# Spectra finished in PSUM: more matmuls and fewer vector steps in the S5 and Hyena stages

## The chip, the cores and the metric

The kernel runs on one core of a Trainium2 chip, which has eight. A core has five engines: PE (TensorE, matrix products, which load their weights in records called PEld), DVE (VectorE), ACT (ScalarE), POOL (GpSimd) and SP (SyncE, which issues most transfers). They run on their own and wait for one another by semaphores; each works off its own instructions strictly in order. Matrix products write to PSUM, from which DVE and ACT read; everything else is in SBUF. The metric is device time in microseconds (us), the median of several runs; profiles come from one execution that the hardware profiler recorded.

## What is computed

Two networks of two layers each run one after the other. Two of their mixers concern the change.

S5 is a diagonal linear recurrence over 512 tokens, 64 groups of 16 features with 64 complex states each:

```
u  = (h @ w_in).reshape(L, 64, 16)
ab = exp((a_re + i a_im) dt);  bb = (ab - 1) / a * b
s[t] = ab * s[t-1] + bb u[t]                 # complex, per group
y  = Re(c s) + d u;  z = gelu(y) @ w_glu
```

Hyena convolves with long filters that a small network of sines makes, scaled by their 1-norms:

```
hid  = sin(freq * (sin(freq * (emb @ w1 + b1)) @ w2 + b2))
h    = (hid @ w3 + b3) * exp(-t * |deltas|)          # forward and backward filters, 2 of each
kern = concat(fwd, 0, reversed(bwd[1:]))             # bwd at lag 0 is left out
k_f  = rfft(kern / sum(|kern|))
for o in range(2):
    z = parts[o + 1] * (irfft(rfft(z) * k_f[o]) + skip[o] * z)
```

## The kernel before

Work is float32 throughout. The projections split each operand into a high and a low part and add three products, in lines 191 to 193; these are most of PE's time. The kernel is written as Python that emits instructions; the order in which it emits them is the order in which each engine runs them, apart from what the framework moves when it places tiles.

**S5** (`s5`, `s5_block`). Eight blocks of 128 features. A block is cut into stages with a letter each: powers of lambda times B and C (`F`, `C`, on POOL through `powers`, tiles tm and pw), a table of unit rotations (`E`, on POOL through `rotation`: four products tm of 128x512, two sums into E), local kernels and the skip term (`Y`, `Z`), chunk inputs on PE (`L`), rotation, scan and rotation back on DVE (`I`, `J`, `K`, tiles rp and rq), outputs on PE (`O`, `U`). A round emits the stages in the order of the string ORDER, and AHEAD says how many blocks a stage runs ahead. The small letters a to h in ORDER are stages of the Hyena filters: two filters a round are worked off between the S5 stages, so that engines idle for the one have the other. S5 rounds run from about 60 to 297 us.

**Filters** (`filters`, stages in `one`). For each of 8 blocks of channels and 2 orders, hid times the sum and the difference of the forward and backward weights (fwpm, made on DVE) gives f + g and f - g in two banks; DVE multiplies them by the decay (ff). At lag 0 only the forward filter counts: three steps on one partition put half the sum into both (lines 1710 to 1712). The 1-norm comes from the larger of the absolute values (fab), summed by PE (line 1723). The skip term is a diagonal matrix fdg, made on DVE and added by PE (line 1734). Then `spectrum` runs, and SP stores the result fX to DRAM.

**`spectrum`** takes four residues (token modulo 4) of 128 channels and gives eight sums: cosine and sine sums of 128 frequencies and their three mirror images. Eight matmuls with the tables dft give the sums of each residue in a pair of banks. ACT copies one bank to spb; DVE makes bank + spb and bank - spb (spt); four more steps of 128x256 combine these into the eight images, on POOL for the filters (fX) and on DVE in Hyena (X). For the filters, whose cosine and sine inputs differ, four matmuls in a third bank give a correction, with a second copy on ACT and a step on DVE.

**Hyena** (`hyena`, `long_conv`), 1942 to 2250 us. PE projects (lines 191 to 193); ACT and DVE do a short convolution; then 8 chains (one for each block of channels, with two convolutions each, so 16 in all) run, two at a time, taken forward by `step` between the projections. A convolution (`long_conv`) is: spectrum X, product with the stored spectrum K (Y and pm; one of the products on POOL), four steps spt<-Y, four steps into a tile that is again named X, and eight inverse matmuls with idft (line 1787). POOL also makes the low parts wl of the projection weights here.

Of the kernel before, what the change touches and what calls it, by code (L numbers as in the profile page):

```python
# [9 lines left out]
F32 = mybir.dt.float32  # L10
# [32 lines left out]
# Stages of the S5 blocks (capitals and w, p, q) and of the Hyena filters among them (a to e, g, h), in the order in  # L43
# which a round emits them; how many blocks a stage is ahead of the round; blocks projected before the first round.
# [5 lines left out]
class Kern:  # L50
# [11 lines left out]
    def psum(self, banks, pairs=0):  # L62
        """PSUM of a phase: single banks and pairs of banks."""
# [36 lines left out]
    def filler(self, ctx, work, banks, pairs=0):  # L100
        """Work emitted in steps among that of a phase; work(pool) is a generator."""
# [51 lines left out]
    def act_table(self, name, after):  # L153
        """Load a table set, after an activation."""
# [60 lines left out]
    def params(self, room, name, groups):  # L215
        """Vectors given as rows of 128, at most 128 of them to a group: loads, then transposes into one tile."""
# [45 lines left out]
    # The operand of a projection is split without 1/rms, which is applied to its output; so it is ready as soon as  # L262
    # the residual is. Sums of squares come out per token, tokens on partitions.
# [27 lines left out]
    def stat_close(self, n=4):  # L291
        """1/rms, [token of block, block]"""
# [6 lines left out]
    def rsqrt(self, r, x):  # L299
        """With a Newton step: the square root is a table's."""  # L300
# [8 lines left out]
    def replicate(self, r4, ps=None):  # L309
        """[P, n] to n * 128 columns, the same on all partitions"""  # L310
# [11 lines left out]
    def ready(self, x, gain, dst):  # L322
        """Split x times gain."""
# [8 lines left out]
    def prepare(self, xT, gain, pool):  # L332
        """For the projections of the next stage: called with each feature block as its residual is final."""
# [16 lines left out]
    def prepare_stat(self, xT):  # L350
        """The statistics alone."""
# [10 lines left out]
    def load_x(self, src, lp):  # L362
        """Input tokens as t = 4 c + j, in halves of the features"""
# [8 lines left out]
    def prepare_x(self, raws, lp):  # L372
        """The residual in natural order into DRAM, the operand in order (j, c)."""
# [61 lines left out]
    def s5_params(self, pp, sp, raw, braw, craw):  # L435
        """Per-state numbers in layout [(g2 p), gp]; B and C in [(g2 p), gp, h]."""
# [13 lines left out]
        # exponentials of a_re dt and four times it; sines and cosines of theta and of 4 theta times 1, 2, 4 ... 64  # L450
# [18 lines left out]
        # f = (lambda - 1) / a  # L469
# [18 lines left out]
        sn, cs, _ = angles(4, 7, self.t([P, 2048], F32, "ssm_b_re", 1, sp).rearrange("p (i c) -> p i c", i=4))  # L488
        # bbar [P, 2, gp, h]
# [14 lines left out]
        # c [P, 2, gp, h]  # L504
# [9 lines left out]
        # powers of lambda, up and down  # L514
        up, down = self.t([P, 2, 32, 5], F32, "up", 1, pp), self.t([P, 2, 32, 4], F32, "down", 1, pp)
        V.memset(up[:, 0, :, 0:1], 1.0)
        V.memset(up[:, 1, :, 0:1], 0.0)
        V.tensor_copy(up[:, :, :, 1], lam)
        u1, u2 = self.t([P, 2, 32], F32, "u1", 1, sp), self.t([P, 2, 32], F32, "u2", 1, sp)
        for i in range(2, 5):  # L520
# [4 lines left out]
        for i in range(4):  # L525
            self.act(down[:, :, :, i], up[:, :, :, 3 - i], AF.Copy)
# [3 lines left out]
        for n in (16, 8):  # L530
            tab = self.t([P, 2, 32, n], F32, f"tab{n}", 1, pp)
            q1, q2 = (room[:, 1024 * (n == 8) + i * S :][:, :S].rearrange("p (c q m) -> p c q m", c=2, q=32) for i in range(2))
            eng = Pl if n == 16 else V
            if n == 8:
                yield
            Pl.memset(tab[:, 0, :, 0:1], 1.0)
            Pl.memset(tab[:, 1, :, 0:1], 0.0)
            m = 1
            while m < n:
                sh = [P, 2, 32, m]  # L540
                bc = lambda x: x[:, b].unsqueeze(1).unsqueeze(3).to_broadcast(sh)
                with self.tc.issue_after(self.scaled) if n == 8 else nullcontext():
# [8 lines left out]
    def exp(self, sp, out, x, out1=None):  # L551
        """exp to float32's accuracy: 2^k times a polynomial on [-ln 2 / 2, ln 2 / 2]; out1 takes exp - 1"""
# [22 lines left out]
    def sin_cos(self, room, r, sn, cs, cm):  # L575
        """r in [-pi, pi]: sine by its series after folding into [-pi / 2, pi / 2]; cm = cos - 1 = -2 sin^2(r / 2)"""
# [16 lines left out]
    def s5_block(self, sp, fb, slot, sS):  # L593
        """The stages of a block of features"""
# [6 lines left out]
        capr, capi, fpr, fpi, bd = slot  # L601
        b = {}

        # C lambda^tau, tau <= 4, or B lambda^(3 - j), spread block-diagonally over the two groups of the partitions
        def powers(src, tab, n, dst):
            pw = self.t([P, 2, 4 * 5 * 16], F32, "pw", 1, p["pool"])[:, :, : 64 * n].rearrange("p c (q t h) -> p c q t h", q=4, h=16)
            m = [[self.t((P, S), F32, f"tm{i}{c}", 1, p["pool"])[:, : 64 * n].rearrange("p (q t h) -> p q t h", q=4, h=16)
                  for c in range(2)] for i in range(2)]
            sh = [P, 4, n, 16]
# [4 lines left out]
            self.tt(pw[:, 0], m[0][0], m[1][1], ALU.subtract, eng1)  # L614
            self.tt(pw[:, 1], m[0][1], m[1][0], ALU.add, eng1)
# [5 lines left out]
        def powers_f():  # L621
            powers(p["bb"], p["down"], 4, (fpr, fpi))
# [1431 lines left out]
```

## Time and profile before

| | us |
|---|---|
| median of 3 runs | 2312.88 (2309.42 to 2322.04) |
| span of the profiled execution | 2317.0 |
| S5 rounds, first two (60 to 134) | 74 |
| S5 rounds, middle three (134 to 233) | 99 |
| S5, last rounds and the start of the gate's projection (233 to 320) | 87 |
| Hyena convolutions (1961 to 2213) | 252 |

The span is the time from the first to the last instruction of the profiled execution. The views show busy time by engine. A PE row holds matmuls, whose records overlap; PEld holds the weight loads. PEclk is the clock that TensorE was granted, as a share of the full 2.4 GHz. "Idle before" is the time for which an engine stood still ahead of a group of instructions, with what ended it. Lines such as L139 are those of helpers that emit an elementwise step, so the tile names tell the steps apart.

### The profile page before, as it was taken

The page shows a single profiled execution, that of the slowest core. Times are in us where ns is not written, and L with a number is a line of the kernel's source. Part 1 is how long each engine was busy: PE and PEld are TensorE (multiplying, and loading weights), DVE is VectorE, ACT ScalarE, POOL GpSimd, SP SyncE. Part 2 cuts the span into 40 slices and gives each one's busy share as a digit, 9 for nine tenths or more (in the row PEclk, how much of TensorE's full clock was granted, in tenths as well). Part 3 has the DMA queues.
Part 4 walks back from the last instruction along what each step waited for, and adds up shares of the span by engine and source line. Part 5 has one row for each costly group of instructions (what it writes and reads, how often), then busy time and mean ns, then how long its engine had stood idle before and what let it go on. Part 6 is the DMA issues. An engine that isn't in the chain of part 4 may idle for free.

```text
span 2317.0 us, 29751 instructions
## 1 busy us (share of the span) xinstructions
PE 2145.5 (93%) x11700; PEld 1782.3 (77%) x11700; DVE 1535.1 (66%) x2451; ACT 973.1 (42%) x1447; POOL 565.3 (24%) x435
## 2 busy tenths in 40 slices
PE   6789999999999999998999999989899998898797
PEld 5578888788888887766778878878688886777676
DVE  9898974767665545654565676465688663988843
ACT  5443433332233446654343233434478653233232
POOL 4998731000000100000100000321244333334331
PEclk8788999999999999998999999979999999999899
DMA  5121262434442321111243553313000022222221
GB/s 160 56 67 60 72 208 85 131 101 140 152 127 76 107 65 46 37 44 39 91 130 102 159 175 104 104 51 85 28 1 1 19 91 73 91 91 73 73 73 55
DMA packets 194515, 199.36 MB, mean 86 GB/s; under 512 B 15059, under 2 KB 184550, under 8 KB 194311
## 3 DMA queue, kind: packets, MB, share of 16 engines
q1 hardware_dynamic: 179703, 183.11, 25.3%
q10 hardware_dynamic: 14672, 14.35, 2.0%
q8 instruction: 92, 1.51, 0.3%
q14 instruction: 48, 0.39, 0.1%
HBM read 182.75 MB, written 14.68 MB: 85 GB/s over the span
## 4 chain that ended last, share of the span: by engine, by line
PE 67%; DVE 20%; issue 4%; DMA 4%; ACT 3%; POOL 2%; SPq 0%; DVEq 0%; ACTq 0%; POOLq 0%
PE bank L193 15%; PE bank L191 15%; PE bank L192 15%; DVE spt L139 2%; PE sc L1362 2%; PE pair L968 2%; PE pair L946 2%; DVE X L139 2%; DVE wl L139 2%; DVE Y L139 1%; DMA wraw<-in_ffn_w_up_dram 1%; ACT wh L151 1%; PE so L1523 1%; PE obank L1787 1%; PE sc L1503 1%
## 5 line engine op out<-in xcount | busy, mean ns | idle before, releaser
L191 PE MATMUL bank<-hh,wh 128*128 128x512 f32 x1472 | 595.2, 405 | 15.8 <-DVE v L142 7.2
L193 PE MATMUL bank<-hh,wl 128*128 128x512 f32 x1472 | 591.8, 402 | 12.9 <-DVE wl L139 12.9
L192 PE MATMUL bank<-hl,wh 128*128 128x512 f32 x1472 | 590.3, 401 | 0.4 <-DVE hl L142 0.4
L151 ACT ACTIVATE wh<-wraw 128x1024 fp32r<-128x1024 f32 (+2 forms) x260 | 244.9, 961 | 358.4 <-PE bank L192 192.7
L139 POOL TENSOR_TENSOR sqa<-sqa,sq 128x512 f32<-128x512 f32 x47 | 70.1, 1491 | 1208.7 <-ACT sq L151 1208.7
L193 PEld LDWEIGHTS bank<-hh,wl 128*128 128x128 f32 x1472 | 283.9, 193 | 81.9 <-DVE wl L139 17.1
L191 PEld LDWEIGHTS bank<-hh,wh 128*128 128x128 f32 x1472 | 283.8, 193 | 81.1 <-issue 8.9
L192 PEld LDWEIGHTS bank<-hl,wh 128*128 128x128 f32 x1472 | 283.8, 193 | 63.1 <-DVE hl L142 2.0
L139 DVE TENSOR_TENSOR wl<-wraw,wh 128x1024 fp32r<-128x1024 f32 (+2 forms) x220 | 242.9, 1121 | 109.7 <-ACT wh L151 109.0
L139 POOL TENSOR_TENSOR wl<-wraw,wh 128x1024 fp32r<-128x1024 f32 x40 | 103.0, 2593 | 171.8 <-ACT wh L151 164.0
L191 PE MATMUL bank<-ah,wh 128*128 128x512 f32 x352 | 138.2, 393 | 0.8 <-ACT wh L151 0.8
L193 PE MATMUL bank<-ah,wl 128*128 128x512 f32 x352 | 137.0, 392 | 1.0 <-DVE wl L139 1.0
L192 PE MATMUL bank<-al,wh 128*128 128x512 f32 x352 | 137.1, 389 | 0.0
L139 DVE TENSOR_TENSOR fg<-bank,rn 128x512 f32<-128x512 f32 x76 | 52.4, 689 | 106.1 <-PE bank L193 104.4
L139 POOL TENSOR_TENSOR sl<-sp,wh 128x768 fp32r<-128x768 f32 x32 | 60.4, 1889 | 113.0 <-ACT wh L151 62.8
L142 DVE SCALAR_TENSOR_TENSOR adaaccx<-adaraw,silc,adaaccx 128x256 f32<-128x256 f32 x168 | 80.7, 481 | 2.2
L193 PEld LDWEIGHTS bank<-ah,wl 128*128 128x128 f32 x352 | 66.0, 188 | 17.1 <-DVE wl L139 3.4
L191 PEld LDWEIGHTS bank<-ah,wh 128*128 128x128 f32 x352 | 66.1, 188 | 15.0 <-ACT wh L151 1.9
L192 PEld LDWEIGHTS bank<-al,wh 128*128 128x128 f32 x352 | 66.1, 188 | 13.6
L142 DVE SCALAR_TENSOR_TENSOR fy<-fg,prm,fy 128x511 f32<-128x511 f32 x88 | 65.9, 749 | 13.9 <-ACT fy L151 12.7
L1787 PE MATMUL obank<-X,idft 128*128 128x128 f32 x256 | 44.0, 330 | 32.6 <-DVE X L139 30.1
L139 POOL TENSOR_TENSOR fX<-spt 128x256 f32<-128x256 f32 x64 | 64.7, 1038 | 30.9 <-DVE spt L139 30.9
(551 smaller groups left out, 4450.5 us busy)
## 6 DMA issues: line engine op xcount, KB each, us to landing
wraw<-in_ffn_w_up_dram SPq DMA_DIRECT2D x88, 512.0 KB
adaraw<-in_ada_w_dram SPq DMA_DIRECT2D x24, 1024.0 KB
wraw<-in_ffn_w_down_dram SPq DMA_DIRECT2D x48, 384.0 KB
wraw<-in_hy_w_in_dram SPq DMA_DIRECT2D x32, 512.0 KB
wraw<-in_attn_w_in_dram SPq DMA_DIRECT2D x18, 512.0 KB
kspec<-fX SPq DMA_DIRECT2D x16, 512.0 KB
wraw<-in_ssm_w_glu_dram SPq DMA_DIRECT2D x16, 512.0 KB
wraw<-in_kv_w_dram SPq DMA_DIRECT2D x16, 512.0 KB
```

Source lines behind the costliest of these rows:

```text
L139: (eng or self.nc.vector).tensor_tensor(out=out, in0=a, in1=b, op=op)
L142: self.nc.vector.scalar_tensor_tensor(out=out, in0=a, scalar=s, in1=b, op0=op0, op1=op1)
L151: return self.nc.scalar.activation(out, a, func, bias=bias, scale=scale, **k)
L191: mm(out, wh[k], xh, start=first and k == 0, stop=False)
L192: mm(out, wh[k], xl, start=False, stop=False)
L193: mm(out, wl[k], xh, start=False, stop=last and k == n - 1)
L946: mm(o, lhs[r, ks], rhs[r, q0:], start=False, stop=True, skip_group_check=True)
L968: mm(z[:, h, c0 + qq - q0 : c0 + S - q0], lhs, t[:, h, cc : cc + n], start=False, stop=True, skip_group_check=True)
L1362: mm(s, l, m[:, c], start=i == 0 and k % 2 == 0, stop=True, skip_group_check=True)
L1503: mm(s[:, k], ones, rows[u], start=False, stop=True, skip_group_check=True)
L1523: mm(o, vh, hi[:, k], start=k == 0, stop=False)
L1787: nc.tensor.matmul(ps[:, r * P : r * P + P], self.idft[:, j, r], Q[:, r, j], start=j == 0, stop=j == 1)
```

## The change

1. `spectrum` adds up each of its eight sums within PSUM: 16 matmuls of 128x128 with a table of 12 matrices, four of them negated copies, instead of 8 matmuls (and 4 more for the filters). Bank 1 is filled first and copied by ACT while bank 0 is filled. Two steps on DVE, bank + spb and bank - spb, write the spectrum. The steps on spt, the third bank and its copy are gone. The images stand in another order.
2. `long_conv` follows that order: the products take strided views, spt<-Y is two steps of 128x512 instead of four of 128x256, and the last four steps write cosine and sine halves of a tile [2, 4] instead of one residue each. spt has one buffer instead of two.
3. `filters`: the lag-0 repair is a matmul of one column (forward weights times hid at token 0) whose result corrects the norm and goes into the skip diagonal. The diagonal moves from DVE to ACT, and its matmul has 256 columns, for two sums. The weight sums move from DVE to POOL; the weights fw have three buffers instead of one.
4. `powers` leaves out the trivial power and copies it instead (n - 1 of n powers, plus a copy on POOL); `rotation` computes only the upper half of the table (128x256 instead of 128x512) and ACT mirrors it, with the sine negated, into the lower half. E is held in two fixed tiles.

The diff without comments and docstrings, cut to these parts:

```diff
...
-        def powers(src, tab, n, dst):
+        def powers(src, tab, n, plain, dst):
...
-            sh = [P, 4, n, 16]
+            sh = [P, 4, n - 1, 16]
+            ts = slice(1, n) if plain == 0 else slice(0, n - 1)
...
-            self.tt(pw[:, 0], m[0][0], m[1][1], ALU.subtract, eng1)
-            self.tt(pw[:, 1], m[0][1], m[1][0], ALU.add, eng1)
+            Pl.tensor_copy(pw[:, :, :, plain], src[:, :, g])
+            self.tt(pw[:, 0, :, ts], m[0][0], m[1][1], ALU.subtract, eng1)
+            self.tt(pw[:, 1, :, ts], m[0][1], m[1][0], ALU.add, eng1)
...
-                    self.tt(t[i][c], fine[:, c, g].unsqueeze(2).to_broadcast([P, 4, 8, 16]),
-                            coarse[:, i, g].unsqueeze(3).to_broadcast([P, 4, 8, 16]), ALU.mult, eng)
-            self.tt(E[:, 0], t[0][0], t[1][1], ALU.subtract, eng1)
-            self.tt(E[:, 1], t[0][1], t[1][0], ALU.add, eng1)
+                    self.tt(t[i][c], fine[:, c, g].unsqueeze(2).to_broadcast([P, 4, 4, 16]),
+                            coarse[:, i, g].unsqueeze(3).to_broadcast([P, 4, 4, 16]), ALU.mult, eng)
+            far = [E[:, i, :, 64:].rearrange("p q (a b) -> p q a b", b=16) for i in range(2)]
+            self.tt(far[0], t[0][0], t[1][1], ALU.subtract, eng1)
+            self.tt(far[1], t[0][1], t[1][0], ALU.add, eng1)
+            self.act(E[:, 0, :, 0:63], E[:, 0, :, 126:63:-1], AF.Copy)
+            self.act(E[:, 1, :, 0:63], E[:, 1, :, 126:63:-1], AF.Copy, scale=-1.0)
...
-    def spectrum(self, pool, xc, xs, X, bufs=2, more=None, eng=None):
+    def spectrum(self, pool, xc, xs, X, bufs=2, more=None):
...
-        for r in range(4):
-            r = 3 - r
-            last = not (more and r == 0)
-            mm(v(r // 2)[:, 3 - r % 2], self.dft[:, 1, r], xs[:, r], start=True, stop=True)
-            mm(v(r // 2)[:, r % 2], self.dft[:, 0, r], xc[:, r], start=True, stop=last)
+        C, S_ = range(4), range(4, 8)
+        C2n, C3n, S3n, S0n = range(8, 12)
+        terms = [(1, 0, C[1], xc, 1), (1, 0, C[3], xc, 3), (1, 1, S_[1], xc, 1), (1, 1, S3n, xc, 3),
+                 (1, 2, S_[1], xs, 1), (1, 2, S_[3], xs, 3), (1, 3, S0n, xs, 0), (1, 3, S_[2], xs, 2),
+                 (0, 0, C[0], xc, 0), (0, 0, C[2], xc, 2), (0, 1, C[0], xc, 0), (0, 1, C2n, xc, 2),
+                 (0, 2, S_[0], xs, 0), (0, 2, S_[2], xs, 2), (0, 3, C[1], xs, 1), (0, 3, C3n, xs, 3)]
+        for i, (bank, place, tab, x, r) in enumerate(terms):
+            mm(v[bank][:, place], self.dft[:, tab], x[:, r], start=i % 8 == 0, stop=True, skip_group_check=True)
+            if i == 7:
+                b = self.t([P, 4, n], F32, "spb", bufs, pool)
+                self.act(b, v[1], AF.Copy)
         if more:
-            more(v(0)[:, 0])
-        b = self.t([P, 4, n], F32, "spb", bufs, pool)
-        self.act(b, v(1), AF.Copy)
+            more(v[0][:, 0:2])
         yield
-        t = self.t([P, 2, 4, n], F32, "spt", 2, pool)
-        self.tt(t[:, 0], v(0), b, ALU.add)
-        self.tt(t[:, 1], v(0), b, ALU.subtract)
-        u, d = t[:, 0], t[:, 1]
-        if xc is not xs:
...
-            self.tt(d[:, 1:3], ps[:, 0:2], b[:, 0:2], ALU.subtract)
-        self.tt(X[:, 0:8:4], u[:, 0:4:3], u[:, 1:3], ALU.add, eng)
-        self.tt(X[:, 1:8:4], u[:, 0:4:3], u[:, 1:3], ALU.subtract, eng)
-        self.tt(X[:, 3:7:3], d[:, 0:2], d[:, 2:4], ALU.add, eng)
-        self.tt(X[:, 2:8:5], d[:, 0:2], d[:, 2:4], ALU.subtract, eng)
+        self.tt(X[:, 0:4], v[0], b, ALU.add)
+        self.tt(X[:, 4:8], v[0], b, ALU.subtract)
...
-                self.tt(wpm[0][:, i], w[0][:, 0:4:2], w[0][:, 1:4:2], op)
+                self.tt(wpm[0][:, i], w[cb][:, 0:4:2], w[cb][:, 1:4:2], op, nc.gpsimd)
...
-            self.tt(xc[0:1, 0], xc[0:1, 0], xs[0:1, 0], ALU.add)
-            self.ts(xc[0:1, 0], xc[0:1, 0], 0.5)
-            nc.vector.tensor_copy(xs[0:1, 0], xc[0:1, 0])
...
+            nc.tensor.matmul(ps[:, 1:2], w[cb][:, 2 * o + 1], hid[:, 0:1], start=True, stop=True)
             yield
             q = slice(8 * o + cb, 8 * o + cb + 1)
-            nc.vector.reciprocal(self.rn[:, q], ps[:, 0:1])
-            n = self.t([P, 1], F32, "fn", 2, fp)
-            self.tt(n, ps[:, 0:1], self.prm[f"skip{o}"][:, cb : cb + 1], ALU.mult)
+            n = self.t([P, 3], F32, "fn", 2, fp)
+            self.act(n[:, 0:1], ps[:, 1:2], AF.Abs)
+            self.tt(n[:, 1:2], ps[:, 0:1], n[:, 0:1], ALU.subtract)
+            nc.vector.reciprocal(self.rn[:, q], n[:, 1:2])
+            self.stt(n[:, 2:3], n[:, 1:2], self.prm[f"skip{o}"][:, cb : cb + 1], ps[:, 1:2], ALU.mult, ALU.subtract)
             dg = self.t([P, P], F32, "fdg", 1, fp)
-            self.ts(dg, self.ident, n)
+            self.act(dg, self.ident, AF.Copy, scale=n[:, 2:3])
...
-        T = self.t([P, 8, P], F32, "spt", 2, pool)
-        self.tt(T[:, 0:2], Y[:, 0:8:4], Y[:, 1:8:4], ALU.add)
...
-        Q = self.t([P, 4, 2, P], F32, "X", 2, pool)
-        self.tt(Q[:, 0], T[:, 0:2], T[:, 4:8:3], ALU.add)
...
+        T = self.t([P, 8, P], F32, "spt", 1, pool)
+        self.tt(T[:, 0:4], Y[:, 0:4], Y[:, 4:8], ALU.add)
+        self.tt(T[:, 4:8], Y[:, 0:4], Y[:, 4:8], ALU.subtract)
+        Q = self.t([P, 2, 4, P], F32, "X", 2, pool)
+        self.tt(Q[:, 0, 0:2], T[:, 0:5:4], T[:, 1:4:2], ALU.add)
+        self.tt(Q[:, 0, 2:4], T[:, 0:5:4], T[:, 1:4:2], ALU.subtract)
+        self.tt(Q[:, 1, 1:3], T[:, 6:1:-4], T[:, 5:8:2], ALU.add)
+        self.tt(Q[:, 1, 3::-3], T[:, 6:1:-4], T[:, 5:8:2], ALU.subtract)
...
```

How PE's instructions stand now, at the two places that the sum speaks of. First an S5 round, before: the end of a filter's spectrum (pair is its two banks, ff the filter with its decay, fdg the skip diagonal, the second bank the correction).

```order
L1621 MATMUL pair_1855<-ff_345_1683,dftf 128x128
L1622 MATMUL pair_1855<-ff_344_1681,dftf 128x128
L1734 MATMUL pair_1855<-fdg_1766,ones 128x128
L1635 MATMUL bank_1870<-ff_345_1683,dftf 128x128
L1636 MATMUL bank_1870<-ff_344_1681,dftf 128x128
```

In the kernel after, at the same place, with outputs of the S5 block (obank<-sS,capr) around:

```order
L716 MATMUL obank_1798<-sS,capr_235 32x128
L1638 MATMUL pair_1850<-ff_334_1681,dftf 128x128 x4
L1638 MATMUL pair_1850<-ff_335_1683,dftf 128x128 x4
L1736 MATMUL pair_1850<-fdg_1762,ones 128x256
L716 MATMUL obank_1798<-sS,capr_235 32x128 x3
```

The correction's matmuls in a bank of their own are gone; the spectrum is written in groups of four, and the block's output matmuls stand between them and behind them.

Next the Hyena stage, before: inverse matmuls of one chain (obank<-X,idft), the projection (bank<-hh,wh and the like) and the start of the other chain's spectrum (pair<-z,dft).

```order
L1787 MATMUL obank_16184<-X_16158,idft 128x128 x2
L191 MATMUL bank_16195<-hh_15793,wh_16106 128x512
L1787 MATMUL obank_16184<-X_16158,idft 128x128 x6
L192 MATMUL bank_16195<-hl_15794,wh_16106 128x512
L193 MATMUL bank_16195<-hh_15793,wl_16107 128x512
L191 MATMUL bank_16195<-hh_15799,wh_16106 128x512
L192 MATMUL bank_16195<-hl_15800,wh_16106 128x512
L193 MATMUL bank_16195<-hh_15799,wl_16107 128x512
L191 MATMUL bank_16284<-hh_15757,wh_16274 128x512
L192 MATMUL bank_16284<-hl_15758,wh_16274 128x512
L1621 MATMUL pair_16245<-z_16193,dft 128x128
```

In the kernel after, at a place of the same kind:

```order
L1638 MATMUL pair_16036<-u_2435_15979,dft 128x128 x8
L1790 MATMUL obank_16057<-X_16028,idft 128x128
L191 MATMUL bank_16078<-hh_15715,wh_16068 128x512
L192 MATMUL bank_16078<-hl_15716,wh_16068 128x512
L193 MATMUL bank_16078<-hh_15715,wl_16069 128x512
L191 MATMUL bank_16078<-hh_15721,wh_16068 128x512
L1790 MATMUL obank_16057<-X_16028,idft 128x128
L1638 MATMUL pair_16036<-u_2435_15979,dft 128x128 x8
L1790 MATMUL obank_16057<-X_16028,idft 128x128 x6
L192 MATMUL bank_16078<-hl_15722,wh_16068 128x512
```

Before, the inverse matmuls stand among projections, with the next spectrum behind them in one piece. Now the spectrum comes in two halves of eight, and the second stands behind the first inverse matmuls of the other chain.

## Rows read from the trace of the kernel before

**Rows 1.** Busy share per engine (tenths) in 40 equal slices, the page.

```profile
PE   6789999999999999998999999989899998898797
DVE  9898974767665545654565676465688663988843
POOL 4998731000000100000100000321244333334331
```

**Rows 2.** Busy time (instructions) by stretch; columns: stretch, length, five engines, granted clock, DMA.

```profile
60.00:134.00 74.00, 52.41 (x344) 38.95 (x344) 64.62 (x69) 33.61 (x63) 69.88 (x63) 0.77 0.20 58
134.00:233.00 99.00, 90.03 (x745) 79.43 (x743) 90.97 (x138) 40.42 (x82) 92.09 (x87) 0.88 0.21 64
233.00:320.00 87.00, 81.31 (x760) 74.61 (x761) 78.20 (x142) 37.23 (x71) 55.39 (x54) 0.92 0.35 121
1961.00:2213.00 252.00, 217.67 (x1168) 185.34 (x1167) 212.75 (x352) 69.94 (x96) 92.21 (x45) 0.93 0.25 79
```

**Rows 3.** The same view, one late S5 round alone.

```profile
257.00:279.00 22.00, 21.33 (x204) 19.67 (x203) 19.92 (x37) 8.87 (x19) 11.50 (x13) 0.84 0.28 97
```

**Rows 4.** POOL groups, 60 to 134 us: busy, mean ns | idle before.

```profile
L139 POOL TENSOR_TENSOR tm<-tab,tab 128x512 f32<-128x512 f32 x16 | 20.5, 1307 | 0.0
L139 POOL TENSOR_TENSOR tm<-cc,up 128x320 f32<-128x320 f32 x9 | 16.3, 1838 | 0.0
L139 POOL TENSOR_TENSOR tm<-bb,down 128x256 f32<-128x256 f32 x16 | 13.2, 854 | 3.4 <-DVE pw L139 3.3
L139 POOL TENSOR_TENSOR E<-tm,tm 128x512 f32<-128x512 f32 x6 | 12.7, 2140 | 0.0
```

**Rows 5.** Busy time of POOL's fX instructions alone, by stretch.

```profile
134.00:233.00 99.00, 25.44 (x25) 0.88 0.21 64
233.00:320.00 87.00, 38.58 (x40) 0.92 0.35 121
```

**Rows 6.** DVE groups of the filters, 60 to 320 us.

```profile
L139 DVE TENSOR_TENSOR ff<-ff,ff 1x128 f32<-1x128 f32 x16 | 10.6, 661 | 0.1
L146 DVE TENSOR_SCALAR fdg<-ident,fn 128x128 f32<-128x128 f32 x16 | 9.6, 602 | 0.1
L139 DVE TENSOR_TENSOR fwpm<-fw 65x256 f32<-65x256 f32 x16 | 7.2, 451 | 0.0
L1712 DVE COPY ff<-ff 1x128 f32<-1x128 f32 x16 | 6.7, 419 | 0.1
L139 DVE TENSOR_TENSOR spt<-bank,spb 128x256 f32<-128x256 f32 x16 | 6.6, 411 | 0.5 <-ACT spb L151 0.5
L146 DVE TENSOR_SCALAR ff<-ff 1x128 f32<-1x128 f32 x16 | 6.2, 385 | 0.1
L139 DVE TENSOR_TENSOR fn<-bank,prm 128x1 f32<-128x1 f32 x16 | 2.2, 136 | 0.0
```

**Rows 7.** Timeline of PE, one spectrum: start, length, instruction.

```profile
2005.74 0.38 PE L1621 MATMUL pair<-z,dft 128*128 128x128 f32 x2
...
2007.30 0.39 PE L1622 MATMUL pair<-z,dft 128*128 128x128 f32 x2
```

**Rows 8.** Groups in the Hyena convolutions, 1961 to 2213 us.

```profile
L139 DVE TENSOR_TENSOR X<-spt 128x256 f32<-128x256 f32 x128 | 60.7, 533 | 0.3
L139 DVE TENSOR_TENSOR Y<-X,K 128x512 f32<-128x512 f32 x32 | 33.7, 1087 | 0.1
L139 DVE TENSOR_TENSOR spt<-Y 128x256 f32<-128x256 f32 x64 | 31.3, 549 | 0.4
```

**Rows 9.** PE's waits there: us in total, times, longest.

```profile
PE obank L1787 <- DVE X L139: 30.1, 10, 6.4
```

**Rows 10.** Timelines of DVE, then POOL, within one convolution.

```profile
2114.58 6.72 DVE L139 TENSOR_TENSOR X<-spt 128x256 f32<-128x256 f32 x4
2122.41 1.42 DVE L139 TENSOR_TENSOR X<-spt 128x256 f32<-128x256 f32 x4
2115.64 5.03 POOL L139 TENSOR_TENSOR wl<-wraw,wh 128x1024 fp32r<-128x1024 f32 x2
```

More of the change, by code (lines that the diff above doesn't have):

```diff
@@ L513, in s5_params @@
                     self.act(cc[r, i, 16 * v : 16 * v + 16], ps[r].rearrange("p (q g h) -> p q g h", g=2, h=16)[:, :, g], AF.Copy)
[L515 to L518, printed above, removed]
+        up, down = self.t([P, 2, 32, 4], F32, "up", 1, pp), self.t([P, 2, 32, 3], F32, "down", 1, pp)
+        V.tensor_copy(up[:, :, :, 0], lam)
         u1, u2 = self.t([P, 2, 32], F32, "u1", 1, sp), self.t([P, 2, 32], F32, "u2", 1, sp)
-        for i in range(2, 5):
+        for i in range(1, 4):
             for u, c in ((u1, 0), (u2, 1)):
@@ L524, in s5_params @@
             self.tt(up[:, 1, :, i], u1[:, 1], u2[:, 0], ALU.add)
-        for i in range(4):
-            self.act(down[:, :, :, i], up[:, :, :, 3 - i], AF.Copy)
+        for i in range(3):
+            self.act(down[:, :, :, i], up[:, :, :, 2 - i], AF.Copy)
         tabs, b = [], 0
         room = self.t([P, 2048], F32, "ssm_b_im", 1, sp)
-        for n in (16, 8):
+        for n in (16, 4):
             tab = self.t([P, 2, 32, n], F32, f"tab{n}", 1, pp)
-            q1, q2 = (room[:, 1024 * (n == 8) + i * S :][:, :S].rearrange("p (c q m) -> p c q m", c=2, q=32) for i in range(2))
+            q1, q2 = (room[:, 1024 * (n == 4) + i * S :][:, :S].rearrange("p (c q m) -> p c q m", c=2, q=32) for i in range(2))
             eng = Pl if n == 16 else V
-            if n == 8:
+            if n == 4:
                 yield
-            Pl.memset(tab[:, 0, :, 0:1], 1.0)
-            Pl.memset(tab[:, 1, :, 0:1], 0.0)
+                Pl.memset(tab[:, 0, :, 0:1], 1.0)
+                Pl.memset(tab[:, 1, :, 0:1], 0.0)
+            else:
+                Pl.tensor_copy(tab[:, 0, :, 0], cs[:, 0])
+                Pl.tensor_copy(tab[:, 1, :, 0], sn[:, 0])
             m = 1
@@ L541, in s5_params @@
                 bc = lambda x: x[:, b].unsqueeze(1).unsqueeze(3).to_broadcast(sh)
-                with self.tc.issue_after(self.scaled) if n == 8 else nullcontext():
+                with self.tc.issue_after(self.scaled) if n == 4 else nullcontext():
                     self.tt(q1[:, :, :, :m], tab[:, :, :, :m], bc(cs), ALU.mult, eng)
@@ L621, in powers_f @@
         def powers_f():
-            powers(p["bb"], p["down"], 4, (fpr, fpi))
+            powers(p["bb"], p["down"], 4, 3, (fpr, fpi))
         def powers_c():
-            powers(p["cc"], p["up"], 5, (capr, capi))
+            powers(p["cc"], p["up"], 5, 0, (capr, capi))
         def transpose_f():
@@ L757, in s5 @@
             with self.sbuf("s5") as sp:
-                blocks = [self.s5_block(sp, fb, self.slots[fb % 2], self.sS) for fb in range(KB)]
+                E = [sp.tile([P, 2, 4, P], F32, name=f"E{i}") for i in range(2)]
+                for t in E:
+                    for i in range(2):
+                        self.nc.gpsimd.memset(t[:, i, :, 63:64], 1.0 - i)
+                blocks = [self.s5_block(sp, fb, (*self.slots[fb % 2], E[fb % 2]), self.sS) for fb in range(KB)]
                 self.y = []
@@ L1609, in reduce_angle @@
         self.ts(r, r, math.pi, -math.pi, ALU.min, ALU.max)
[L1611 removed]
+    def spectrum(self, pool, xc, xs, X, bufs=2, more=None):
         n = xc.shape[-1]
         ps = self.pair()
[L1616 removed]
+        v = [ps[:, i].rearrange("p (a c) -> p a c", a=4) for i in range(2)]
         mm = self.nc.tensor.matmul
[L1618 to L1622 removed]
+        C, S_ = range(4), range(4, 8)
[9 more added lines that the diff above has]
+                self.act(b, v[1], AF.Copy)
@@ L1649, in filters @@
         self.rn = self.const.tile([P, 16], F32, name="rnorm")
-        self.dft = fp.tile([P, 2, 4, P], F32, name="dftf")
+        self.dft = fp.tile([P, 12, P], F32, name="dftf")
         nc.sync.dma_start(self.dft, a["hy_dft"])
@@ L1786, in long_conv @@
             for j in range(2):
-                nc.tensor.matmul(ps[:, r * P : r * P + P], self.idft[:, j, r], Q[:, r, j], start=j == 0, stop=j == 1)
+                nc.tensor.matmul(ps[:, r * P : r * P + P], self.idft[:, j, r], Q[:, j, r], start=j == 0, stop=j == 1)
         return ps
@@ L1801, in hyena @@
         with self.sbuf("hy") as hp:
-            self.dft = hp.tile([P, 2, 4, P], F32, name="dft")
+            self.dft = hp.tile([P, 12, P], F32, name="dft")
             nc.scalar.dma_start(self.dft, a["hy_dft"])
```

55 lines of the change are left out of this document (22 added, 33 removed).

## The prediction

> **What bounds the kernel now.** I read the page's slices first, to see which stages have an engine that is never free [rows 1]. Two do where the change works: the S5 stage at the left (slices 2 to 6), where PE, DVE and POOL are all high, and the Hyena stage near the right (slices 35 to 38), where PE and DVE are. Between them lies code that the change leaves alone, so the sum is made of these two stages. Then I cut each into stretches and read the busy time of every engine [rows 2]. From 60 to 134 us POOL works 69.88 of 74.00 us while PE works 52.41: POOL sets the pace. From 134 to 233 us three engines are within 3 us of each other (POOL 92.09, DVE 90.97, PE 90.03 of 99.00); relief of one alone gives nothing there. From 233 to 320 us PE leads with 81.31 of 87.00, and a single late round shows PE busy for 21.33 of 22.00 us [rows 3]. In the Hyena convolutions, 252.00 us, PE is busy 217.67 and DVE 212.75 [rows 2], and nearly all the rest of PE's time is one wait: the inverse transform for DVE's last write, 30.1 us in 10 pieces [rows 9]. The granted clock in these four stretches is 0.77, 0.88, 0.92 and 0.93 on average [rows 2]: TensorE is part of the time at the lower of its two levels, 1.2 GHz, and mostly at 2.4.
>
> **The prices.** One spectrum of before is eight matmuls of 128x128; they start at 2005.74 and the eighth at 2007.30, so seven steps take 1.56 us and one costs 0.223 us at the full clock [rows 7]. At half the clock I take twice that, an estimate.
>
> A filter's spectrum now has 16 such matmuls instead of 8 + 4; the skip term's matmul has 256 columns instead of 128 (one more 0.223), and the lag-0 repair is one matmul of one column, at most 0.223 by the same row. Six times 0.223 is 1.3 us of PE for each of 16 filters, 21 us in all. A Hyena convolution has 16 instead of 8: 1.78 us for each of 16 convolutions, 28.5 us.
>
> What DVE is rid of in the filters: three one-partition steps for lag 0 (10.6 + 6.2 + 6.7 us), the skip diagonal (9.6, to ACT), the weight sums (7.2, to POOL) and the correction from the third bank (6.6): 46.9 us for 16 filters [rows 6]. It gets two steps of one column in their place, 0.136 us each by the row of fn, some 4 us. Net: 43 us. The two additions that read PSUM stay, with another target.
>
> What POOL is rid of: fX, 25.44 us and 38.58 us in the two stretches that have it [rows 5], and part of the tables. From 60 to 134 us [rows 4] half of tm<-tab (20.5) and of E (12.7) goes, a fifth of tm<-cc (16.3) and a quarter of tm<-bb (13.2): 10.2 + 6.3 + 3.3 + 3.3 = 23.1 us. The copies that come in are half as long as a tm<-bb of 874 ns; six of them make 2.6 us. Net 20.5 of 69.88.
>
> ACT takes over the mirrored half of E, the skip diagonal and |f| at lag 0. It is busy for 33.61 of 74.00, 40.42 of 99.00 and 37.23 of 87.00 us [rows 2], and the tables are made a round ahead; I cost this at nothing. Were it exposed, two mirror copies a block would stand before the rotation; I leave 0.5 us a block, 4 us, in the range. The larger dftf load lies in the prologue on SP; no transfer was late there for PE, and I cost it at nothing too.
>
> **S5, stretch by stretch.** *60 to 134 us.* POOL falls to about 49 of 74, and DVE with 64.62 is next. That alone frees 74.00 − 64.62 = 9.4 us. DVE's own instructions also get shorter, since the two engines shut each other out: four writes that otherwise take 1.42 us took 6.72 us while POOL ran two wl of 5.03 us [rows 10]. The ends are 0 (another chain, such as the filters' sine, sets the end) and −20.5 (all of POOL's saving); I take −12, nearer to DVE's row.
>
> *134 to 233 us.* 25 of 64 fX lie here, so about 6.25 filters. POOL loses 25.4 and some 0.29 (20.5 of 69.88) of the other 66.7, and gets six weight sums of at most 0.9 us: to about 53. DVE loses 6.25/16 of 43 = 17, to 74. PE gains 6.25 × 1.3 = 8, to 98 of 99 if the clock stays at 0.88. So PE takes over at once, and the gain hangs on the clock: PE's 98 us scaled by 0.88 to a full clock are 86.5. Ends 0 and −12.5. PE that waits less for DVE and POOL should be granted more, so I take −8, two thirds of the way.
>
> *233 to 320 us.* Ten filters add 13.3 us to PE: 94.6 where there are 87.00, and PE had next to no gap in the late rounds [rows 3]. With 0.92 scaled to a full clock they are 87.0. Ends 0 and +7.6; I take +3, since DVE loses 27 us here and the gaps at the start of the stretch go.
>
> In the code's order the S5 outputs now stand between the two halves of a filter's spectrum on PE; what they wait for (capr, sS) is old by then, so I cost that at nothing; were it late, a filter would wait, not the block.
>
> Sum for S5: −12 − 8 + 3 = −17 us, ends −33 and +8 (+12 with the mirror copies).
>
> **Hyena.** DVE loses the four short steps of each forward spectrum, half of the 128 instructions of X<-spt: 30.4 us of 60.7. Its 64 spt<-Y (31.3 us) become 32 of twice the width; by Y<-X,K of that shape, 1.087 us and less where POOL is quiet, they cost about the same. DVE falls from 212.75 to about 182 [rows 8]. PE rises from 217.67 by 28.5 to 246 of 252.00. So the bound changes hands. What the stretch then takes is 246 us plus the gaps that stay. Now there are 34.3 us of them, 30.1 of it the wait for X in 10 pieces [rows 9]. DVE's way to that wait is shorter by four short steps, about 2 us, so 20 us of it should go. But two things work against it. The four last steps of the product now put all residues into two halves of one tile, so the first inverse matmul waits for the last of them, where it waited residue by residue. And PE's row shows the second half of the other chain's spectrum behind the first inverse matmuls: while PE waits for one chain, the other's spectrum is held up too. I take 16 us of gaps: 246 + 16 = 262, +10 us. Ends: no gap left, −6; all gaps left, 246 + 34.3 = 280.5, +28.5. The first end would need PE to work 252 us through without one wait, the second that four steps less on DVE shorten none, so the middle is likelier than either.
>
> **Sum.** −17 + 10 = −7. The profiled execution's own span is 2317.0 us, within the three timed runs (2309.42 to 2322.04, median 2312.88); it would go to 2310. Against the median I forecast **2306 us**. The ends added up are −39 and +40, to be reached by chance together only.
>
> **Rivals.** *PE has more room than its busy row says.* Speaking for it: PE's records overlap and its clock is below full in every stretch; both stages have DVE at 84% or more, and DVE is relieved by 43 + 30 us. If PE's additions find room, S5 gives 28 us (close to the end of −33) and Hyena 5 (246 us less 15, since 0.93 leaves up to 7% to a full clock, plus gaps of 16): −33, **2280 us**. Against it: PE was busy 21.33 of 22.00 us in a late round. [...] Chance 0.27.
>
> *The other side: PE and DVE wait for each other in Hyena.* The place is the second half of a spectrum behind the other chain's first inverse matmuls. DVE has nothing to add until that half is through, and PE does not get to it before DVE's last write. Price: the inverse's eight matmuls and the half's eight, 16 × 0.223 = 3.6 us of DVE idle, in three of four convolutions (12): 43 us. DVE's 182 + 43 = 225, plus its other idle of before (252.00 − 212.75 = 39) and the steps around the sets, gives up to 264 to 280; it decides from the point where PE's own work behind the spectrum is shorter than DVE's share of a convolution (182 / 16, some 11 us). With Hyena at +28 and S5 at only −8: +20, **2333 us**. Against: PE still has projections to put in. Chance 0.20.
>
> *Nothing in sum: PE is the bound in both, and the change only swaps engines.* S5 gives 10 (the first stretch alone), Hyena takes 10: **2313 us**. Here the relief of DVE and POOL brings nothing behind 134 us. Chance 0.13.
>
> **How the numbers follow.** 0.40 for the forecast (own range 2297 to 2316), 0.27, 0.20 and 0.13. A measurement of this kernel can tell about 0.5%, 11.6 us, from no change. Faster than 2301.3: the first rival and a quarter of the forecast, 0.37. Slower than 2324.4: the second, 0.20. Within: 0.43. The range goes from 2281 to 2331; below lies a bit less than half of the first rival, above half of the second, together 0.2.
>
> **What would show it.** Right: POOL under 55 of the first 74 us and that stretch 10 us shorter; PE over 95% busy in the rounds behind it at a clock above 0.88; lag-0 steps gone from DVE; in Hyena PE busy near 246, its wait for X near 12 us, DVE near 182. Wrong: a first stretch that stays at 74 (then a chain other than POOL's set it); Hyena under 250 (the first rival) or over 275 with DVE idle before X<-pair (the second); a clock that falls where PE has more to do.

## The result, and the profile of the kernel after

The kernel became slower: 2349.6 us (2345.74 to 2360.33, 4 runs) against 2314.36 us for before, a ratio of 1.015 with a 95% interval of 1.0126 to 1.0174. I had forecast 2306 and a range up to 2331. The profiled execution of after, the slowest of the four, has a span of 2358.6 us, 41.6 more than that of before. Cut at the first load of GLU weights (307.8 us before, 305.4 after), at the first load of Hyena weights (1911.0, 1915.0), at the first forward matmul (1974.6, 1979.8) and at the end of the last inverse one (2211.5, 2249.6), the difference is −2.4 us up to the end of S5, +6.3 in the middle, +1.2 ahead of the convolutions, **+33.0 in the convolutions** and +3.5 behind them. The middle runs the same instructions in both kernels; in the traces of all kernels here it takes between 1592.8 and 1609.6 us (1592.8 in the run with S5 new and Hyena old), so I take its 6.3 us for scatter.

The stretches of after that answer to [rows 2], in the same columns; the convolutions with their borders, 252 us before, now take 286:

```profile
60.00:134.00 74.00, 53.28 (x374) 40.44 (x375) 55.01 (x68) 41.03 (x79) 57.87 (x74) 0.79 0.23 65
134.00:233.00 99.00, 91.46 (x821) 81.62 (x820) 64.28 (x103) 43.64 (x92) 42.46 (x71) 0.97 0.23 72
233.00:320.00 87.00, 82.89 (x797) 74.68 (x797) 55.38 (x93) 36.47 (x74) 16.67 (x22) 1.00 0.32 110
1965.00:2251.00 286.00, 246.19 (x1409) 214.95 (x1409) 196.19 (x256) 67.82 (x93) 88.70 (x44) 0.93 0.23 70
```

In S5, POOL and DVE are relieved (POOL less than I had counted in the first 74 us, 57.87 where I had put 49, and more behind them), and from 134 us on TensorE is granted nearly the full clock; yet the stage ends where it did. In the convolutions PE is busy for 246.19 us, the 246 of the sum, but 39.8 us of gaps are left where I took 16. The waits there, first of PE (answering to [rows 9]), then of DVE:

```profile
PE obank L1790 <- DVE X L139: 33.6, 13, 5.6
PE pair L1638 <- DVE z L139: 3.7, 2, 2.9
...
DVE X L139 <- PE pair L1638: 54.6, 16, 12.4
```

Before, DVE's wait at that place was 13.4 us in 4 (for ACT's spb). Now DVE stands still for PE in every convolution, and PE for DVE in most: the two wait for each other. One such place, PE first, then DVE (a 128x128 matmul of this kernel leaves two records, so x16 is one half of a spectrum, eight matmuls):

```profile
2019.67 1.95 PE L1638 MATMUL pair<-z,dft 128*128 128x128 f32 x16
2021.45 0.39 PE L1790 MATMUL obank<-X,idft 128*128 128x128 f32 x2
2026.16 2.50 PE L1790 MATMUL obank<-X,idft 128*128 128x128 f32 x10 [4.32 <-DVE X L139]
2028.46 3.02 PE L1638 MATMUL pair<-z,dft 128*128 128x128 f32 x16
...
2020.38 5.73 DVE L139 TENSOR_TENSOR X<-spt 128x256 f32<-128x256 f32 x4
2031.59 1.29 DVE L139 TENSOR_TENSOR X<-pair,spb 128x512 f32<-128x512 f32 x2 [4.03 <-PE pair L1638]
```

The first half of a spectrum is through at 2021.6. PE then stands 4.32 us at an inverse matmul until DVE has written X. Only behind it comes the second half (2028.46 to 2031.48), at a granted clock of 0.53 from 2026 to 2031 us, after the pause, and DVE, which has nothing else left, waits 4.03 us for that.

The built program shows why. These are PE's instructions there with their waits:

```
L1638 MATMUL pair_16206<-z_16156,dft 128x128 [waits DVE_49]
L1638 MATMUL pair_16206<-z_16156,dft 128x128 x7
L1790 MATMUL obank_16227<-X_16198,idft 128x128 [waits DVE_49,PE_49]
L1790 MATMUL obank_16227<-X_16198,idft 128x128 [waits DVE_49]
L1790 MATMUL obank_16227<-X_16198,idft 128x128 x4
L1638 MATMUL pair_16206<-z_16156,dft 128x128 [waits Activation_49]
L1638 MATMUL pair_16206<-z_16156,dft 128x128 x7
```

The ninth matmul waits for ACT, which copies bank 1 out of the tile while the ninth writes bank 0 of the same tile. The data doesn't need this: the framework guards the tile as a whole (with two tiles this wait is gone, as the experiments show). In the gap it put other matmuls, in 9 of 16 spectra the other chain's inverse matmuls among them.

### The profile page after: what moved, and what is told of

Its sections match the earlier page's. It is cut to its first block, busy times and chain, and to the rows that moved or that the text cites. A ratio compares the mean times of both kernels' runs of the same rounds, so it can differ in the third digit from the quotient of the medians.

```text
span 2358.6 us, 30430 instructions
## 1 busy us (share of the span) xinstructions
PE 2183.8 (93%) x12116; PEld 1820.6 (77%) x12116; DVE 1457.5 (62%) x2268; ACT 983.3 (42%) x1480; POOL 459.1 (19%) x407
## 4 chain that ended last, share of the span: by engine, by line
PE 72%; DVE 13%; DMA 4%; issue 3%; ACT 3%; POOL 3%; SPq 0%; DVEq 0%; ACTq 0%; POOLq 0%
PE bank L191 15%; PE bank L193 15%; PE bank L192 15%; PE pair L1638 4%; PE sc L1373 2%; DVE X L139 2%; PE pair L979 2%; PE pair L957 2%; DVE wl L139 1%; DMA wraw<-in_ffn_w_up_dram 1%; DMA adaraw<-in_ada_w_dram 1%; POOL tm L139 1%; DVE Y L139 1%; ACT wh L151 1%; PE obank L1790 1%
## 5 line engine op out<-in xcount | busy, mean ns | idle before, releaser
L193 PEld LDWEIGHTS bank<-hh,wl 128*128 128x128 f32 x1472 | 280.7, 191 | 77.3 <-DVE wl L139 14.9
L192 PEld LDWEIGHTS bank<-al,wh 128*128 128x128 f32 x352 | 66.1, 188 | 13.4
L1638 PE MATMUL pair<-ff,dftf 128*128 128x128 f32 x512 | 66.0, 281 | 9.3 <-ACT fn L151 4.0
```

Source lines behind the costliest of these rows:

```text
L192: mm(out, wh[k], xl, start=False, stop=False)
L193: mm(out, wl[k], xh, start=False, stop=last and k == n - 1)
L1638: mm(v[bank][:, place], self.dft[:, tab], x[:, r], start=i % 8 == 0, stop=True, skip_group_check=True)
```

## The experiments

Medians of before beside the runs: 2314.36 us for after, then 2316.12 for the next four, 2314.57 for the four behind them, 2315.82 for the last four. "Convolutions" is the time from the first forward matmul to the end of the last inverse one in the trace, "S5 end" the first load of GLU weights.

| kernel | median us | ratio to before (95%) | convolutions | S5 end |
|---|---|---|---|---|
| before | | | 236.8 | 307.8 |
| after | 2349.6 | 1.0126 to 1.0174 | 269.8 | 305.4 |
| S5 new, Hyena old | 2310.7 | 0.9966 to 1.0005 | 236.6 | 304.9 |
| S5 old, Hyena new | 2351.5 | 1.0125 to 1.0186 | 269.0 | 308.3 |
| after, two tiles | 2308.8 | 0.9946 to 0.9994 | 231.2 | 300.1 |
| after, copy last | 2324.2 | 1.0016 to 1.0048 | 252.4 | 296.8 |
| before, forward matmuls twice | 2345.3 | 1.0118 to 1.0162 | 263.5 | 309.5 |
| before, short tables | 2309.4 | 0.9957 to 0.9992 | 236.6 | 307.8 |
| before, repair | 2326.7 | 1.0033 to 1.0079 | 235.5 | 324.1 |
| after, copy last in S5, two tiles in Hyena | 2304.2 | 0.9935 to 0.9968 | 230.7 | 296.2 |
| after, inverse behind | 2330.2 | 1.0033 to 1.0068 | 245.2 | 305.8 |
| before, repair, sums on DVE | 2317.9 | 0.9997 to 1.0029 | 236.6 | 312.2 |
| before, one spt | 2323.2 | 1.0005 to 1.0034 | 237.1 | 314.5 |
| the mended kernel, other order of X | 2303.4 | 0.9928 to 0.9968 | 228.5 | 292.8 |

**Which stage (two runs).** One keeps `spectrum` and `long_conv` of before for Hyena, with the filters stored in the old order of images; the other is the reverse.

```diff
-        for _ in self.spectrum(pool, u, u, X):
+        for _ in self.spectrum_old(pool, u, u, X):
```

> The S5 stage and the filters as in the kernel after, the Hyena convolutions as in the kernel before (their spectra of eight matmuls and six vector steps). Theory A, the whole loss of 35 us lies in the Hyena convolutions (their stretch went from 252 to 286 us) and S5 is about neutral: the first GLU weights issue at 305 to 306 us as in the kernel after, and the time is 2308 to 2316 us. Rival B, the relieved S5 stage also delays what follows it (the middle of the program drifted by 6 us between the two traces): 2320 us or more.

> The S5 stage and the filters as in the kernel before (with the filters' spectra stored in the new order of images), the Hyena convolutions as in the kernel after. Theory A: the loss is all here, 2346 to 2352 us, with the stretch of the convolutions at 284 to 288 us. Rival B: part of the loss belongs to S5 and its outcome, 2330 to 2340 us.

Measured 2310.7 and 2351.5, with the convolutions at 236.6 and 269.0. The loss is all in Hyena, and S5 is about neutral.

**The split (two runs).** Two tiles instead of one, or the copy behind all matmuls:

```diff
-        ps = self.pair()
-        v = [ps[:, i].rearrange("p (a c) -> p a c", a=4) for i in range(2)]
+        v = [self.ps2.tile([P, S], F32, tag=f"half{i}", name=self.nm(f"half{i}")).rearrange("p (a c) -> p a c", a=4) for i in range(2)]
...
-            if i == 7:
-                b = self.t([P, 4, n], F32, "spb", bufs, pool)
-                self.act(b, v[1], AF.Copy)
+        b = self.t([P, 4, n], F32, "spb", bufs, pool)
+        self.act(b, v[1], AF.Copy)
```

> The kernel after, with the two halves of a spectrum in two PSUM tiles of one bank each instead of one tile of two banks. In the kernel after the first matmul of the second half waits for ACT, which copies the first half out of the same tile, and the scheduler has put the other chain's inverse matmuls into that gap. Theory C, most of the loss is that split (DVE waited 54.6 us in 16 waits for the second half): the 16 matmuls stand together, DVE's waits for the spectrum fall below 25 us, the Hyena stretch comes down from 286 to about 262 us and the time to 2320 to 2330 us. Rival D, the loss is the 28 us of added PE work, wherever it stands: 2340 us or more.

> The kernel after, with ACT's copy of the first bank emitted behind all 16 matmuls of a spectrum, so that no matmul waits for it; the copy (about 0.6 us) then stands between the last matmul and DVE's first step. Theory C: as with two tiles, but later by up to 0.6 us in each of 16 convolutions: 2322 to 2338 us. Rival D: 2345 us or more.

With two tiles the ninth matmul no longer waits for ACT and all 16 stand together in each of the 16 spectra; 40.8 us of the median are gone, more than theory C asked for, and the convolutions are 5.6 us shorter than before's. DVE's and PE's waits for each other are less than half of after's:

```profile
DVE X L139 <- PE half L1637: 26.9, 10, 12.4
...
PE obank L1789 <- DVE X L139: 14.0, 9, 3.2
```

With the copy last the 16 also stand together, but the way from the last matmul to DVE's first step leads over ACT (DVE's wait for spb is 28.7 us in 10), and the convolutions take 21.2 us longer than with two tiles. The time is within the range, but that is more than the 0.6 us for each of 16 that I had allowed for the copy.

**The price of PE's work alone.** Before, each forward matmul of Hyena issued twice:

```diff
+            for _ in range(2 if xc is xs else 1):
```

> The kernel before, with each of the eight forward matmuls of a Hyena spectrum issued twice (the second writes the same sum again), so PE has the 128 matmuls that the change adds there, in one piece and with no wait of their own, and DVE keeps all its steps. Theory F, PE's added work alone has little room: the Hyena stretch grows by half or more of 28 us, 2330 to 2345 us. Rival G, the added work fits into the gaps in which PE waited for DVE (34 us in 252): at most 8 us, below 2325 us.

2345.3 us, at the upper end of theory F: the convolutions grow by 26.7 of the 28.5 us that the matmuls cost by the price of [rows 7]. PE's waits for DVE hardly give way to the new work (30.1 us before [rows 9]):

```profile
PE obank L1788 <- DVE X L139: 27.1, 12, 4.9
```

The runs make a ladder: 236.8 before; 263.5 with the matmuls added; 252.4 with DVE's short steps gone as well (copy last); 231.2 with the copy beside the second half (two tiles); 269.8 with the same copy in one tile. Work on PE lengthens the stretch and work taken from DVE shortens it: neither engine alone sets it, but the chain that runs through both.

The convolutions alone show where the time lies, in the columns of [rows 2]: before, after, matmuls twice, two tiles.

```profile
1974.63:2211.47 236.84, 202.51 (x1099) 173.36 (x1099) 209.24 (x348) 63.63 (x88) 85.96 (x41) 0.93 0.25 78
1979.83:2249.62 269.79, 229.98 (x1336) 201.93 (x1336) 192.67 (x252) 62.44 (x86) 82.38 (x41) 0.92 0.23 69
1972.06:2235.57 263.51, 230.03 (x1338) 202.68 (x1338) 212.30 (x348) 63.41 (x86) 82.03 (x41) 0.91 0.22 70
1963.60:2194.78 231.18, 215.12 (x1332) 190.45 (x1332) 180.79 (x252) 62.62 (x86) 83.33 (x41) 0.97 0.26 80
```

PE's gaps are 34.3, 39.8, 33.5 and 16.1 us. Between after and two tiles, with the same matmuls, 23.7 of the 38.6 us are gaps; the other 14.9 are PE's busy time, which is shorter at a clock of 0.97 than at 0.92.

**Wait or order.** The inverse matmuls are held behind the last spectrum emitted; tile, halves and the wait for ACT stay as in after; four to ten other matmuls stand between the halves.

```diff
+        with self.tc.issue_after(self.spectral.ins):
             for r in range(4):
```

> The kernel after, with each chain's inverse matmuls held behind the last spectrum that was emitted. A spectrum still stands in two halves with four to seven projection matmuls between them and its second half still waits for ACT, but no inverse matmul, which waits for DVE, stands ahead of a second half any more (in the kernel after it does in 9 of 16). Theory J, that coupling is the loss: the Hyena convolutions take 232 to 246 us from the first spectrum to the last inverse matmul (269.8 in the kernel after, 231.2 with two tiles), 2308 to 2326 us. Rival K, the wait for ACT and the longer way to DVE's first step are the loss: 258 us or more, 2338 us or more.

Convolutions 245.2 us, within theory J's 232 to 246; the median of 2330.2 is 4 us over its range and 19.4 under after. Of the 38.6 us between one tile and two, 24.6 go with the order alone, and 14.0 stay with the wait for ACT and the matmuls between the halves.

```profile
DVE X L139 <- PE pair L1638: 29.5, 10, 12.5
...
PE obank L1791 <- DVE X L139: 20.7, 9, 4.4
```

**S5, one relief at a time.** First the short tables alone (`powers`, `rotation`), then the lag-0 repair, diagonal and weight sums alone, the latter also with the sums left on DVE. For room the two with the repair have one buffer of spt in the filters, which a fourth run has alone.

```diff
-                self.tt(wpm[0][:, i], w[cb][:, 0:4:2], w[cb][:, 1:4:2], op, nc.gpsimd)
+                self.tt(wpm[0][:, i], w[cb][:, 0:4:2], w[cb][:, 1:4:2], op)
...
-        t = self.t([P, 2, 4, n], F32, "spt", 2, pool)
+        t = self.t([P, 2, 4, n], F32, "spt", 2 if xc is xs else 1, pool)
```

> The kernel before with the shorter tables of S5 alone (powers without the trivial one, the rotation table half mirrored); filters, spectra and Hyena as before. Theory H, POOL sets the pace of the first rounds and its relief is worth some 10 us: the first GLU weights issue at 296 to 300 us (307.8 before), 2304 to 2308 us. Rival I, another chain ends the rounds and the tables alone give less than 3 us: 2312 to 2318 us.

> The kernel before with the filters' lag-0 repair by a matmul, the skip diagonal on ACT and the weight sums on POOL; spectra of eight matmuls and the vector steps as before, with one buffer of the sums spt in the filters instead of two (for room). DVE is rid of some 36 us in S5, PE gets 16 matmuls of one column. Theory H2, DVE's relief is worth 3 to 8 us in the middle rounds: 2308 to 2313 us. Rival I2, POOL takes the time back (its weight sums are 13 us more work on an engine that is full): 2314 us or more.

> As the run with the lag-0 repair alone (2326.7 us), but with the weight sums left on DVE, so that POOL gets no work. Theory I2, the sums on a full POOL were the loss: back to 2308 to 2316 us and the first GLU weights at 303 to 309 us (324.1 with the sums on POOL). Rival L, the longer chain PE, ACT, DVE, DVE, ACT, PE of the repair or the single buffer of spt is the loss: 2320 us or more.

> The kernel before with one buffer instead of two for the sums spt in the filters, as both runs on the repair have it. If POOL's late reading of spt holds DVE up: 2320 us or more and the first GLU weights at 315 us or later. If not: 2310 to 2318 us.

The tables alone: 2309.4 us, between the two theories; in the trace the second round ends at 126.9 us instead of 134.1, but the third at 172.0 instead of 168.9, and S5 ends at 307.8 as before. The repair with the sums on POOL loses 12 us; with the sums on DVE it is level with before (2317.9, between its two theories). POOL, full in these rounds, was no place for the sums while the tables and fX were still on it. The single spt costs a little by itself (2323.2 us, ratio 1.002, S5 end 314.5, just short of the 315 named), so the repair on DVE may be worth a few us with two buffers; that wasn't run.

**A version that beats both.** Copy last for the filters, two tiles for Hyena; then the same with DVE's last four steps in another order.

> The kernel after, with the filters' spectra as in the run where the copy comes last and the Hyena spectra in two tiles of one bank each. If the two stages add up (S5 11 us and Hyena 5 us shorter than before by their traces), 2296 to 2304 us; if the gain of the S5 stage in that run was chance, 2306 to 2310 us.

> As the run with both stages mended (2304.2 us), with the last four vector steps of a convolution in another order, so that the first residue is complete after two of them. PE waited 14.0 us in 9 waits for these steps; if the first inverse matmuls then start up to 0.7 us earlier in each of 16 convolutions, 2294 to 2303 us; if PE merely waits at the third residue, 2302 to 2307 us.

2304.2 us, at the edge of the range for stages that add up, ratio 0.9935 to 0.9968: 10 us faster than before and 45 faster than after. The other order gives 2303.4, in the range for no gain; the two can't be told apart.

## Why the prediction was wrong, point by point

- **Prices of matmuls and counts: right, at the clock of before.** PE's 246 us in Hyena were forecast to the microsecond, and the fX, lag-0 and diagonal steps went as counted. (A slip that changes nothing: a tm<-bb took 854 ns in [rows 4]; 874 is its mean from 60 to 320 us.) Inside the convolutions PE's busy time rose by 27.5 us in after and with the matmuls doubled (28.5 forecast), at clocks of 0.92 and 0.91; with two tiles, at 0.97, by 12.6 only.
- **The gaps in Hyena: the step that failed.** I took 16 us of gaps since DVE's way was shorter by four steps, and set the likeliest between the ends. They are 39.8. I had named both halves of the mechanism, PE's second half behind the first inverse matmuls and DVE idle until it is through, and priced it as the second rival: +28 us in Hyena, chance 0.20, its sign a stretch of over 275 us with DVE idle before X<-pair. It was the case: 286 us, +33.0 in the convolutions. With that row of the order in hand, a middle value was wrong: what stood ahead of the second half was an instruction known from [rows 9] to be PE's main wait. Without the guard on the tile, the 16 us did come: 16.1 with two tiles.
- **The second rival's price: near in part by luck.** I had 43 us of DVE idle, 3.6 us in each of 12 places; DVE's wait for the spectrum rose from 13.4 to 54.6, by 41. But in the trace of after the 9 spectra with an inverse matmul between their halves hold 27.0 of the 54.6 us, 3.0 each, and the other 7 hold 27.6. Nearly as much stays with the inverse matmuls behind (29.5) and with two tiles (26.9). And what opened the gap between the halves, the ninth matmul's wait for ACT, I had not named at all.
- **"The bound changes hands": wrong as a model.** I added busy times as if the busier engine set the stretch. Doubling the forward matmuls cost 26.7 of 28.5 us where PE had 34 us of gaps: added work on the chain found no room in them. The Trainium skill (Perfetto Trace Analysis, "Identifying the Most-Contended Engine") says to judge TensorE's headroom by MFU (the share of its peak arithmetic) and the busy share of weight loads, not by matmul busy time. By the weight loads (185.34 of 252.00 us [rows 2]) an estimate of the room is 66 us; this run found 1.8.
- **The first rival: wrong for the change as written, right in Hyena once the tile is split.** It put Hyena at −5: 246 us less 15 by the clock, plus 16 of gaps. Two tiles have just that: 14.9 us less PE busy time than after, 16.1 of gaps, convolutions 5.6 us shorter than before's. The room that it claimed was in the clock and in PE's waits, and the two halves of a spectrum kept both out of reach. Its 28 us in S5 came in no run (15.0 at most).
- **DVE at 182: it was 196.** One kind of step became slower: X<-spt of after against [rows 8] has half the count for nearly the same time. spt<-Y went the other way, to 21.5 us where I had left 31.3. The last row is POOL beside the four writes shown above:

```profile
L139 DVE TENSOR_TENSOR X<-spt 128x256 f32<-128x256 f32 x64 | 56.5, 933 | 0.7
L139 DVE TENSOR_TENSOR spt<-Y 128x512 f32<-128x512 f32 x32 | 21.5, 711 | 0.5
...
2020.76 5.07 POOL L139 TENSOR_TENSOR wl<-wraw,wh 128x1024 fp32r<-128x1024 f32 x2 [4.10 <-ACT wh L151]
```

  The four writes that PE waits for took 5.73 us at 2020.38 while POOL ran two wl, as four took 6.72 us in [rows 10]. In the trace of before 8 of the 128 X<-spt (5 of them among the 64 last writes) are longer than 0.8 us and overlap a wl, 17.4 us in all; of the 64 of after 16 are, 37.9 us, and with two tiles 9, 20.9 us. I had let the steps that stay keep their mean; the last writes went from 561 to 933 ns. No run takes the wl away, so that the overlap is the cause is read from traces alone.
- **S5: −17 forecast, −2.4 measured.** By the starts of ACT's gelu of each block: up to the end of the second round −10.7 (−12 forecast); rounds three to five +6.8 (−8 forecast); from there to the GLU +1.5 (+3 forecast). The middle term failed. It hung on a full clock, which did come (0.97 over the stretch), but its first round, the third of all, went from 34.8 to 45.3 us. Part of this is a shift of work: PE has 143 records in the second round instead of 175, and 320 in the third instead of 272, so the gain of the first term came back in the second; both rounds together take 67.7 us, before 69.0. Busy times of 15 us of the third round, in after and then in the run with the copy last:

```profile
138.00:153.00 15.00, 12.00 (x71) 11.22 (x70) 6.70 (x13) 4.91 (x11) 9.22 (x16) 0.78 0.26 80
138.00:153.00 15.00, 14.76 (x108) 12.93 (x107) 11.90 (x18) 4.46 (x11) 7.67 (x13) 1.00 0.31 98
```

  ACT's new work, which I had costed at nothing, stands in PE's pause there. From 123 to 169 us, DVE's wait for the norm's correction on ACT, and ACT's for POOL ahead of the mirror copies:

```profile
DVE fn L139 <- ACT fn L151: 6.9, 3, 4.3
...
ACT E L151 <- POOL dec L656: 5.5, 1, 5.5
```

  On ACT |f| stood behind E, E behind a POOL that now had the weight sums ahead of its tables, and PE's next filter (line 1703) behind the norm, for which PE waited 3.0 us. The cover named, "a round ahead", didn't hold here.

  That this chain is what lengthened the round is not shown. Two more traces with the same S5 stages (S5 new with Hyena old, where fX alone is stored in another order, and inverse behind) have 42.1 and 42.5 us, with the same 3.0 us of wait but a clock of 0.92 instead of 0.85. The tables alone, with neither |f| on ACT nor the sums on POOL, have 45.1 us, two tiles 48.8. With the copy last the round, with the same 320 records, takes 38.3 us: PE is busy for 36.34 us at 0.96 instead of 40.98 at 0.85. S5 then ends 11 us earlier than before; how much of that is the split and how much the other order around it, the runs don't separate. What set the middle rounds of after stays open.
- **No relief alone gives anything in the middle rounds: not contradicted.** The tables alone end S5 where it was (307.8). The repair with the sums on DVE ends it at 312.2, 2.3 us earlier than the single spt that it shares does alone; with two buffers it wasn't run.

## What to carry to other kernels

When work is added to an engine with gaps, ask whether it lies on the chain that makes the gaps: if it does, count it nearly in full (26.7 of 28.5 us here), whatever the busy shares leave free. When two engines share a tile in pieces, check what the framework guards: one wait that the data doesn't need was worth 40 us here, and 24.6 of the 38.6 us in the convolutions went with what was put in front of the waiting instruction. In a row of instructions, anything that stands behind a known long wait is to be priced with that wait. When one round becomes shorter, count the instructions of the next one too before calling it a gain.

## What the runs showed of the hardware that I had not expected

PE's pauses showed in the price of its matmuls. Inside the convolutions nearly the same number of records kept PE busy for 229.98 us at a granted clock of 0.92 in after, where it had 39.8 us of gaps, and for 215.12 us at 0.97 with two tiles, where it had 16.1. A pause cost twice there, as a gap and as slower matmuls behind it: the granted clock was 0.53 from 2026 to 2031 us, behind the 4.32 us pause shown above, and 1.00 from 2019 to 2021 us ahead of it.

A higher clock in S5 did not make the stage shorter. From 60 to 320 us PE ran 1992 records instead of 1849, for 227.63 us instead of 223.75, at 0.97 instead of 0.88 in the middle rounds and 1.00 instead of 0.92 behind them, and the stage ended 2.4 us earlier: the clock carried the added matmuls.
